# Half of the weight slabs cast straight from fp32 memory into the SBUF ring, with loads issued five slabs ahead

## The chip, the cores and the metric

The kernel runs on all 8 cores of one Trainium2 chip, one batch element on each core. The metric is the device time of the slowest core in microseconds (us), as the median of several executions. Most executions of one kernel agree within a fraction of a per cent. Some fall into a second, slower state, in which the cores of one die show a lower granted TensorE clock and the time is some per cent longer. A stage is read from the trace of one profiled execution, and where one core of it is named, from that core.

## The reference

The reference is one decoder layer on x of shape (8, 2048, 1024), with fp32 inputs and outputs. Each core gets one batch element, so 2048 rows of 1024.

```python
hcat = x @ w_in                                     # 7 groups of 512 columns
b_gate, c_gate, hc, q, k, v, g = split(hcat)
y_conv = b_gate * causal_short_conv(c_gate * hc, conv_w)
o      = chunkwise_retention(rotary(q), rotary(k) * 128**-0.5, v)   # 4 heads, 128 each
y_ret  = silu(g) * head_group_norm(o)
mix    = concat([y_conv, y_ret]) @ w_out            # 1024 x 1024
x      = layer_norm(alpha * x + mix)
ff     = square(relu(x @ w_ff1)) @ w_ff2            # 1024 x 4096, 4096 x 1024
ple    = sigmoid(x @ w_ple_gate) * (p @ w_ple_proj)
x      = layer_norm(alpha * x + ff + ple)
```

## The kernel before

The program has a conv stage, a retention stage of 18 steps, and then four tiles of 512 rows. A tile runs ff1 (8 weight slabs), gate (2 slabs), the output projection "mix" of the next tile (2 slabs of w_out) and ff2 (8 slabs). A slab is a [128, 8, 512] block of weights: 1 MiB in bf16, 2 MiB in fp32. TensorE works in bf16 and the weights arrive in fp32, so before any slab is loaded, the kernel casts it once from fp32 DRAM to bf16 DRAM scratch. Only DMAs that GpSimd issues (the software queue) cast here; SP issues plain loads (the hardware queue).

```python
casts = []                                   # 20 DRAM-to-DRAM casts, issued by GpSimd
for g in range(2): casts.append((s_wout[g], w_out[g], ("c_wout", g), ("s_wout", g)))
# ... [cut: the same for 8 of ff1, 2 of gate, 8 of ff2]
issue_casts(4)                               # and then one after each retention step

NR = 6                                       # six slabs in the ring
def load_slab(src, rsrc):                    # issued by SP, in order, at the point of use
    i = rcnt[0] % NR
    rcnt[0] += 1
    h.dma("sp", ring[i][:], src, ("ring", i), [rsrc], [("ring", i)])
    return ring[i], ("ring", i)

def mix_part(tt, bi, hf, slab, rs, bank):    # x @ w_out for 128 rows, half the columns
    b = tt * 4 + bi
    i = xcnt[0] % 4                          # four xin buffers of 256 KB
    xcnt[0] += 1
    cols = slice(hf * 512, (hf + 1) * 512)
    h.dma("sp", xin[i][:], x[b * 128:(b + 1) * 128, cols], ("xin", i), [], [("xin", i)])
    for kc in range(8):
        h.mm(ps[bank][:], ycat[:, kc, blk(b)], slab[:, kc, :], kc == 0, kc == 7, ...)
    h.stt(x1v(tt, bi)[:, cols], xin[i][:], ALPHA, ps[bank][:], ALU.mult, ALU.add, ...)

for tt in range(4):
    phase_ff1(tt)
    bg.flush()
    phase_gate(tt)
    if tt < 3:
        phase_mix(tt + 1)                    # two halves hf, four blocks bi each
        bg.add(gen_norm1(tt + 1))            # LayerNorm and transposes, spread over ff2
    phase_ff2(tt)                            # uses the same PSUM banks ps[bi] as phase_mix
    # ... [cut]
```

Tile 0's own mix runs inside the retention stage, in steps 8 to 11, with its own eight xin loads. An xin buffer is loaded again only when VectorE's `stt` of four blocks earlier has read it. And ff2 writes the PSUM banks that the last `stt` of the mix must first have read.

## Time and profile before

The median was 900.96 us when the prediction was made. The profile is of core 0, 896.4 us. In what follows, a stage is bounded by the starts of TensorE's weight loads, counted from the first: all 4,088 are in every trace, in the same order of work, so the same count is the same point of the program.

| | before |
|---|---|
| PE busy | 807.7 us, 90% |
| retention stage (all 18 steps, with the first five ff1 groups) | 200.8 us |
| rest of ff1 of tile 0 | 60.2 us |
| last mix half before ff2, tiles 0, 1, 2 | 9.7, 9.5, 9.6 us |
| from the last matmul's weight load to the end | 19.3 us |

The page's busy time of TensorE (busy us, share of the span, instructions), and its table of DMA queues (packets, MB, share of the time of the 16 DMA engines). q0 is the queue of GpSimd and q1 that of SP:

```profile
PE 807.7 (90%) x4088; PEld 376.8 (42%) x4088; DVE 443.7 (49%) x696; ACT 276.8 (31%) x500; POOL 126.1 (14%) x165
...
q1 hardware_dynamic: 17280, 96.68, 32.9%
q0 software_dynamic: 5136, 41.42, 30.8%
```

TensorE bounds the kernel and has about 89 us of idle time; DMA engines are busy 64% on average. What TensorE waited for (us in total, times, longest us), on core 0:

```profile
PE psT L198 <- DVE ob_94 L201: 24.8, 7, 18.8
PE ps L194 <- DMA wc_59<-wc: 18.3, 1, 18.3
PE ps L194 <- DMA ring_108<-s_ff: 9.6, 2, 7.4
...
PE ps L194 <- DMA ring_106<-s_ff: 2.5, 1, 2.5
PE ps L194 <- DMA ring_104<-s_ff: 2.4, 1, 2.4
```

The 18.3 us is the start, which the change does not touch. The others are the gaps that it can touch: 18.8 us is the prediction's gap A, 7.4 us its gap B, and the 2.2 us beside it (9.6 in two waits), 2.5 and 2.4 us its gaps C. The largest is VectorE's, which works in order and waits for an x load. The timeline shows it (start us, us, engine, line, operation, and in brackets the idle time before it and what ended that):

```profile
116.93 0.95 SPq L236 DMA_DIRECT2D xin_115<-x  x1
...
213.16 0.69 DVE L212 SCALAR_TENSOR_TENSOR xacc_118<-xin_115,ps 128x512 f32<-128x512 f32 x1 [20.71 <-DMA xin_115<-x]
...
215.90 0.58 PE L198 MATMUL psT<-ident,ob_94 128*128 128x128 bf16 x4 [18.75 <-DVE ob_94 L201]
```

A load of 256 KB took from 116.9 to 213 us. Last, three windows at the end of tile 0's gate and mix, core 0 (window, its length, busy us and instructions of PE, PEld, DVE, ACT and POOL, granted clock, share of the DMA engines, GB/s):

```profile
338.00:365.00 27.00, 27.00 (x127) 12.21 (x125) 10.49 (x16) 9.55 (x16) 0.00 (x0) 1.00 0.82 278
365.00:383.00 18.00, 18.00 (x86) 8.16 (x84) 10.97 (x16) 6.21 (x10) 0.00 (x0) 1.00 0.00 1
383.00:400.00 17.00, 14.53 (x68) 6.47 (x67) 8.49 (x15) 0.45 (x1) 0.13 (x1) 1.00 0.56 163
```

Just before the mix the DMA engines do nothing at all (share 0.00): SP stands in its in-order queue before the x loads of the mix and issues nothing behind them. This is the DMA view of 365 to 420 us (KB each, us from issue to landing):

```profile
xin_114<-x SPq DMA_DIRECT2D x1, 256.0 KB, 2.9
xin_115<-x SPq DMA_DIRECT2D x1, 256.0 KB, 4.1
xin_116<-x SPq DMA_DIRECT2D x1, 256.0 KB, 3.8
xin_117<-x SPq DMA_DIRECT2D x1, 256.0 KB, 5.0
```

### The profile page before, as it was taken

The page shows a single profiled execution, that of the slowest core. Times are in us where ns is not written, and L with a number is a line of the kernel's source. Part 1 is how long each engine was busy: PE and PEld are TensorE (multiplying, and loading weights), DVE is VectorE, ACT ScalarE, POOL GpSimd, SP SyncE. Part 2 cuts the span into 40 slices and gives each one's busy share as a digit, 9 for nine tenths or more (in the row PEclk, how much of TensorE's full clock was granted, in tenths as well). Part 3 has the DMA queues.
Part 4 walks back from the last instruction along what each step waited for, and adds up shares of the span by engine and source line. Part 5 has one row for each costly group of instructions (what it writes and reads, how often), then busy time and mean ns, then how long its engine had stood idle before and what let it go on. Part 6 is the DMA issues. An engine that isn't in the chain of part 4 may idle for free.

```text
span 896.4 us, 12614 instructions; the slowest of 8 cores (879.0 to 896.4 us)
## 1 busy us (share of the span) xinstructions
PE 807.7 (90%) x4088; PEld 376.8 (42%) x4088; DVE 443.7 (49%) x696; ACT 276.8 (31%) x500; POOL 126.1 (14%) x165
## 2 busy tenths in 40 slices
PE   1999999973988869989999999999998999999991
PEld 0444444431444324434444443444443444444440
DVE  4559545522765323553358453427655344844143
ACT  2222235541666513302224311214430222432011
POOL 3000045631345300000001000001100000100001
PEclk9999999995999979999999999999999999999996
DMA  8999999994866999058446419435805744643201
GB/s 133 216 170 140 109 201 113 124 112 81 141 118 95 142 220 337 29 173 297 141 150 205 164 28 325 165 141 176 276 18 145 306 154 145 213 169 137 95 24 70
DMA packets 22479, 138.90 MB, mean 155 GB/s; under 512 B 2960, under 2 KB 3088, under 8 KB 10384
## 3 DMA queue, kind: packets, MB, share of 16 engines
q1 hardware_dynamic: 17280, 96.68, 32.9%
q0 software_dynamic: 5136, 41.42, 30.8%
q8 instruction: 34, 0.56, 0.3%
q14 instruction: 29, 0.24, 0.1%
HBM read 162.73 MB, written 29.36 MB: 214 GB/s over the span
## 4 chain that ended last, share of the span: by engine, by line
PE 73%; DMA 8%; DVE 5%; issue 4%; ACT 3%; POOL 3%; another core or an unknown queue 2%; SPq 0%; DVEq 0%; ACTq 0%; POOLq 0%
PE ps L194 71%; DMA ring_108<-s_ff 3%; DMA xT_56<-xT 3%; ACT sqj L223 2%; PE psT L198 1%; POOL st_51 L201 1%; DVE xacc_119 L201 1%; DVE lnst L645 1%; DMA ring_106<-s_ff 1%; DMA ring_104<-s_ff 1%; DVE ra_80 L201 1%; ACT xacc_119 L223 1%; DVE ob_93 L201 0%; DVE ob_94 L201 0%
## 5 line engine op out<-in xcount | busy, mean ns | idle before, releaser
L201 POOL TENSOR_TENSOR lnst<-lnst,neghalf 128x1 f32<-128x1 f32 x32 | 17.8, 556 | 461.7 <-DVE lnst L205 461.7
L223 ACT ACTIVATE xacc_119<-xacc_119,lnst 128x1024 f32<-128x1024 f32 x16 | 19.8, 1236 | 99.2 <-DVE lnst L212 99.2
L201 DVE TENSOR_TENSOR hT<-ps,tR_129 128x512 bf16<-128x512 f32 x42 | 28.9, 688 | 36.2 <-ACT tR_129 L223 36.1
L194 PE MATMUL ps<-ring_104,hT 128*128 128x512 bf16 x192 | 43.1, 379 | 2.4 <-DMA ring_104<-s_ff 2.4
L194 PE MATMUL ps<-ycat,ring_108 128*128 128x512 bf16 x160 | 38.1, 400 | 7.4 <-DMA ring_108<-s_ff 7.4
L201 DVE TENSOR_TENSOR hT<-ps,tR_128 128x512 bf16<-128x512 f32 x43 | 29.6, 689 | 30.3 <-ACT tR_128 L223 30.2
L194 PE MATMUL ps<-ycat,ring_107 128*128 128x512 bf16 x192 | 44.1, 386 | 0.0
L223 ACT ACTIVATE tR_129<-ps 128x512 f32<-128x512 f32 x42 | 25.1, 597 | 61.0 <-PE ps L194 57.5
L194 PE MATMUL ps<-ring_105,hT 128*128 128x512 bf16 x192 | 43.2, 379 | 0.0
L201 DVE TENSOR_TENSOR hT<-ps,tR_127 128x512 bf16<-128x512 f32 x43 | 29.6, 689 | 27.1 <-ACT tR_127 L223 25.6
L194 PE MATMUL ps<-ycat,ring_106 128*128 128x512 bf16 x192 | 42.9, 379 | 0.0
L223 ACT ACTIVATE tR_127<-ps 128x512 f32<-128x512 f32 x43 | 25.7, 597 | 54.3 <-PE ps L194 49.7
L223 ACT ACTIVATE tR_128<-ps 128x512 f32<-128x512 f32 x43 | 25.7, 597 | 53.1 <-PE ps L194 49.6
L194 PE MATMUL ps<-ring_108,hT 128*128 128x512 bf16 x160 | 37.7, 392 | 2.2 <-DMA ring_108<-s_ff 2.2
L194 PE MATMUL ps<-ring_106,hT 128*128 128x512 bf16 x160 | 35.5, 379 | 2.5 <-DMA ring_106<-s_ff 2.5
L201 DVE TENSOR_TENSOR xacc_119<-ps,xacc_119 128x512 f32<-128x512 f32 x16 | 11.0, 690 | 51.6 <-PE ps L194 51.5
L194 PE MATMUL ps<-ring_109,hT 128*128 128x512 bf16 x160 | 36.2, 379 | 0.0
L194 PE MATMUL ps<-ring_107,hT 128*128 128x512 bf16 x160 | 35.7, 379 | 0.0
L194 PE MATMUL ps<-ycat,ring_109 128*128 128x512 bf16 x160 | 35.3, 379 | 0.1
L194 PE MATMUL ps<-ycat,ring_105 128*128 128x512 bf16 x160 | 35.4, 379 | 0.0
L194 PE MATMUL ps<-ycat,ring_104 128*128 128x512 bf16 x160 | 35.3, 379 | 0.0
L223 ACT ACTIVATE ycat<-psT 128x1024 bf16<-128x1024 bf16 x16 | 16.3, 1020 | 58.4 <-PE psT L198 58.4
(254 smaller groups left out, 1440.9 us busy)
## 6 DMA issues: line engine op xcount, KB each, us to landing
s_ff<-w_ff POOLq DMA_DIRECT2D x16, 1024.0 KB, 17.4
ring_106<-s_ff SPq DMA_DIRECT2D x11, 1024.0 KB, 7.8
ring_107<-s_ff SPq DMA_DIRECT2D x11, 1024.0 KB, 7.0
ring_104<-s_ff SPq DMA_DIRECT2D x11, 1024.0 KB, 6.0
ring_105<-s_ff SPq DMA_DIRECT2D x11, 1024.0 KB, 5.4
ring_108<-s_ff SPq DMA_DIRECT2D x10, 1024.0 KB, 6.8
ring_109<-s_ff SPq DMA_DIRECT2D x10, 1024.0 KB, 6.3
out<-xacc_118 POOLq DMA_DIRECT2D x8, 512.0 KB, 6.2
```

Source lines behind the costliest of these rows:

```text
L194: self.P.op("pe", lambda e: e.matmul(out, lhsT=lhsT, rhs=rhs, start=start, stop=stop, skip_group_check=skip), reads, writes)
L198: self.P.op("pe", lambda e: e.transpose(out=out, in_=in_, identity=ident), reads, writes)
L201: self.P.op(eng, lambda e: e.tensor_tensor(out=out, in0=in0, in1=in1, op=op), reads, writes)
L223: self.P.op("act", lambda e: e.activation(out=out, in_=in_, func=func, **kw), reads, writes)
L645: P.op("dve", lambda e, hf=hf: e.bn_stats(out=st6[:, hf * 6:(hf + 1) * 6], in_=buf[:, hf * 512:(hf + 1) * 512]), [rbuf], [rl])
```

## The change

The intent was to halve the DRAM-to-DRAM casts and to keep the ring full. Half of the slabs (even ones) are now cast from fp32 DRAM straight into the ring by GpSimd in every tile. In tile 0 all of them are. Slabs are issued five ahead of their use. The x loads leave `mix_part` and are issued a little earlier: the first four of a tile at its gate stage, each further one when its buffer is free.

```diff
-        casts = []
-        for g in range(2):
-            casts.append((s_wout[g], w_out[g], ("c_wout", g), ("s_wout", g)))
-        ... [cut: ff1, gate, ff2; 20 in all]
+        slab_list = [("wout", g, 0) for g in range(2)]
+        for tt in range(4):
+            slab_list += [("ff1", g, tt) for g in range(8)]
+            slab_list += [("gate", g, tt) for g in range(2)]
+            if tt < 3:
+                slab_list += [("wout", g, tt + 1) for g in range(2)]
+            slab_list += [("ff2", g, tt) for g in range(8)]
+        casts = [(n, g) for n, c in (("ff1", 8), ("gate", 2), ("wout", 2), ("ff2", 8))
+                 for g in range(1, c, 2)]                       # 10 in all
+        def prefetch(upto):
+            while slab_n["load"] < min(upto, len(slab_list)):
+                ...
+                if tt > 0 and g % 2 == 1:
+                    h.dma("sp", ring[i][:], wsrc[nm][1][g], ("ringh", i), [("s_" + nm, g)],
+                          [("ring", i)])
+                else:
+                    cast(ring[i][:], wsrc[nm][0][g], ("ring", i), ("ring", i))
+        def use_slab(nm, g, ahead=5):
+            ...
+            prefetch(k + 1 + ahead)
+            return ring[slab_buf[k]], ("ring", slab_buf[k])
@@ mix_part
-            h.dma("sp", xin[i][:], x[b * 128:(b + 1) * 128, cols], ("xin", i), [], [("xin", i)])
...
+            if xn["use"] % 8 <= 4 and xn["use"] % 8 > 0:
+                load_xin(1)
@@ retention loop
-                slabs0 = [load_slab(s_wout[g], ("s_wout", g)) for g in range(2)]
+                slabs0 = [use_slab("wout", g, 0) for g in range(2)]
+                load_xin(4)
-            issue_casts(1)
+            if t % 2 == 0:
+                issue_casts(1)
@@ phase_gate
-                slab, rs = load_slab(s_gate[hf], ("s_gate", hf))
+                slab, rs = use_slab("gate", hf)
+                if hf == 0:
+                    load_xin(4)
@@ phase_mix, phase_ff1, phase_ff2: load_slab(...) becomes use_slab(...) [cut]
```

More of the change, by code (lines that the diff above doesn't have):

```diff
@@ L429, in build_nc @@
               [("wc", 1)], ["wVf"])
-        casts = []
-        for g in range(2):
-            casts.append((s_wout[g], w_out[g], ("c_wout", g), ("s_wout", g)))
-        for g in range(8):
-            casts.append((s_ff1[g], w_ff1[g], ("c_ff1", g), ("s_ff1", g)))
-        for g in range(2):
-            casts.append((s_gate[g], w_gate[g], ("c_gate", g), ("s_gate", g)))
-        for g in range(8):
-            casts.append((s_ff2[g], w_ff2[g], ("c_ff2", g), ("s_ff2", g)))
+        wsrc = dict(wout=(w_out, s_wout), ff1=(w_ff1, s_ff1), gate=(w_gate, s_gate),
+                    ff2=(w_ff2, s_ff2))
+        slab_list = [("wout", g, 0) for g in range(2)]
[5 more added lines that the diff above has]
+            slab_list += [("ff2", g, tt) for g in range(8)]
+        slab_buf = [0, 1, 2, 3, 0, 1, 4, 5]
+        while len(slab_buf) < len(slab_list):
+            slab_buf.append(slab_buf[-6])
+        casts = [(n, g) for n, c in (("ff1", 8), ("gate", 2), ("wout", 2), ("ff2", 8))
+                 for g in range(1, c, 2)]
         def issue_casts(n):
@@ L443, in issue_casts @@
                 if casts:
-                    cast(*casts.pop(0))
+                    nm, g = casts.pop(0)
+                    cast(wsrc[nm][1][g], wsrc[nm][0][g], ("c_" + nm, g), ("s_" + nm, g))
+        slab_n = {"load": 0, "use": 0}
+        def prefetch(upto):
+            while slab_n["load"] < min(upto, len(slab_list)):
+                k = slab_n["load"]
+                slab_n["load"] += 1
+                nm, g, tt = slab_list[k]
+                i = slab_buf[k]
+                if tt > 0 and g % 2 == 1:
[4 more added lines that the diff above has]
+        def use_slab(nm, g, ahead=5):
+            k = slab_n["use"]
+            slab_n["use"] += 1
+            assert slab_list[k][:2] == (nm, g), (slab_list[k], nm, g)
+            prefetch(k + 1 + ahead)
+            return ring[slab_buf[k]], ("ring", slab_buf[k])
         h.cp("dve", ident[:], identf, ["cst"], ["ident"])
@@ L517, in build_nc @@
         bg.flush()
-        issue_casts(4)
+        prefetch(3)
+        issue_casts(3)
         rot = [0]
@@ L662, in gen_ln, with load_xin @@
             yield
-        xcnt = [0]
+        xorder = [(bi, hf) for bi in range(4) for hf in range(2)]
+        xorder += [(4 * tt + bi, hf) for tt in range(1, 4) for hf in range(2) for bi in range(4)]
+        xn = {"load": 0, "use": 0}
+        def load_xin(k):
+            for _ in range(k):
+                if xn["load"] == len(xorder):
+                    return
+                b, hf = xorder[xn["load"]]
+                i = xn["load"] % 4
+                xn["load"] += 1
+                h.dma("sp", xin[i][:], x[b * 128:(b + 1) * 128, hf * 512:(hf + 1) * 512],
+                      ("xin", i), [], [("xin", i)])
         def x1v(tt, bi):
@@ L673, in mix_part @@
             b = tt * 4 + bi
-            i = xcnt[0] % 4
-            xcnt[0] += 1
+            i = xn["use"] % 4
+            assert xorder[xn["use"]] == (b, hf) and xn["use"] < xn["load"]
+            xn["use"] += 1
             cols = slice(hf * 512, (hf + 1) * 512)
-            h.dma("sp", xin[i][:], x[b * 128:(b + 1) * 128, cols], ("xin", i), [], [("xin", i)])
             for kc in range(8):
@@ L694, in x1_transpose @@
             h.cp("act", ycat[:, :, blk(b)], psT[:], [RT], [("ycat", b)])
-        rcnt = [0]
-        def load_slab(src, rsrc):
-            i = rcnt[0] % NR
-            rcnt[0] += 1
-            h.dma("sp", ring[i][:], src, ("ring", i), [rsrc], [("ring", i)])
-            return ring[i], ("ring", i)
         ff1 = {"n": 0, "slab": None}
@@ L708, in ff1_group @@
             if fc % 4 == 0:
-                ff1["slab"] = load_slab(s_ff1[fc // 4], ("s_ff1", fc // 4))
+                ff1["slab"] = use_slab("ff1", fc // 4, 5 if tt or fc > 4 else 0)
             slab, rs = ff1["slab"]
@@ L774, in build_nc @@
                 bg.add(chains[bi])
-            issue_casts(1)
+            if t == 12:
+                prefetch(6)
+            if t == 16:
+                prefetch(8)
+            if t % 2 == 0:
+                issue_casts(1)
         issue_casts(len(casts))
@@ L820, in phase_mix @@
             for hf in range(2):
-                slab, rs = load_slab(s_wout[hf], ("s_wout", hf))
+                slab, rs = use_slab("wout", hf)
                 for bi in range(4):
@@ L846, in phase_ff2 @@
                 if tt == 3 and hf == 1:
-                    slabs = [load_slab(s_ff2[4 + g], ("s_ff2", 4 + g)) for g in range(4)]
+                    slabs = [use_slab("ff2", 4 + g) for g in range(4)]
                     for bi in range(4):
@@ L855, in phase_ff2 @@
                 for g in range(4):
-                    slab, rs = load_slab(s_ff2[hf * 4 + g], ("s_ff2", hf * 4 + g))
+                    slab, rs = use_slab("ff2", hf * 4 + g)
                     for bi in range(4):
```

## The prediction

> **What bounds it now.** TensorE: busy 90% of 896.4 us (page, part 1), 73% of the chain of waits. A middle tile (446 to 594 us, windows view) has PE busy 145.8 of 148 us, so only gaps can be won. PE's waits on core 0 that the change can touch:
>
> - A: 18.8 us at 197 us. A PE transpose waits for ob_94 because VectorE, in order, waits 20.7 us for xin_115. That 256 KB load was issued at 116.9 us and landed at 213, behind two ring loads on its queue, while software-queue casts kept the DMA share at 1.03 (118 to 193 us). In 110 to 215 us the software queue moved 21 KB a packet (9.67 MB, 455 packets), the hardware queue 3.4 KB. The Trainium skill (DMA: Bandwidth & Descriptors, "Queues, rings and completion order") says each DMA engine round-robins between queues at packet granularity; 96 us for xin_115 agrees.
> - B: 7.4 us at 314 us: the third ff1 slab, issued only at 298.3, landed 22.8 us later behind the backlog.
> - C: 2.5, 2.2 and 2.4 us, one at each ff2 start. The ff2 loads stand behind eight xin loads in SP's in-order queue and go out 8 us before need.
>
> After a gap matmuls run 0.43 us apart instead of 0.216 (timeline, about 12 after B). The skill (TensorE: Matmul & The Clock Gate, "Part 1: The HAM clock gate") describes this half clock when cold. I add 3 us for B and 3 for A and C. Sum: 18.8 + 7.4 + 7.1 + 6 = 39 us on core 0. The same sum puts nearly every core near 855 to 858.
>
> **What the change does.** Removes 10 of 20 DRAM-to-DRAM casts, 9 to 10 us of DMA each (the s_wout casts landed at 86.4 and 96.3 us). Turns 50 of 80 slab loads into fp32 casts on GpSimd's queue: about 6.3 us each (landings of xT_57 to wK, 52.2 to 77.3 us for four), against 3.2 for a bf16 slab (part 3: 32.9% of 896 us for 96.7 MB). Estimate: -95 + 155 = +60 us of DMA work, share 64% to about 74%. None should be critical: PE uses a slab in 6.9 us, five are ahead. Tightest is tile 0: 18 casts x 6.3 = 113 us, plus about 18 for pT, wproj, ln2, xin = 131 of 147 us. Moved: xin goes ahead of need and no longer before ring loads; the wout slabs leave SP's queue; slab waits now sit in GpSimd's in-order stream beside the LayerNorm powers.
>
> **On the critical path:** A, B and C go. I charge 3 us for new waits. Start (18.3 us before the first matmul), conv stage, retention steps (about 9.4 us each) and the 30 us LayerNorm tail stay.
>
> **Predicted: 863 us, 80% range 852 to 880.** Faster by over 2%: 0.90; within 2%: 0.08; slower: 0.02.
>
> **Right if:** no VectorE wait for xin near 193 us, no PE wait for ring tiles at ff1 and ff2 starts, PE busy 93 to 94%, software-queue share up and hardware-queue share down, cores' spans closer together. **Wrong if:** PE waits for ring tiles in tile 0 (casts slower than 6.9 us with both cores of a pair reading 2 MB a slab); PE transposes wait on LayerNorm chains delayed at GpSimd; xin still lands after step 8 because the remaining casts saturate the queue; or the granted clock falls as PE becomes denser.

## The result and the profile after

The changed kernel took 892.9 us in the median of 10 runs, against 899.37 us in 20 runs of the kernel before (three slow runs are in the first median, one in the second). The ratio of the fast runs is 0.9922, with a 95% interval of 0.9901 to 0.9943. Such a ratio is the mean time of one kernel's fast runs over that of the other's of the same rounds, so it is not quite the ratio of the medians quoted. The change is real and under 1%, and outside the predicted range of 852 to 880. The profiled execution's slowest core is core 4, 891.7 us.

The ledger by stages shows that the expected gains came, nearly all of them, and that they were given back mostly in one place.

```
stage (us)                          before, core 0   after, core 4   difference
retention (gap A in it)                     200.8           180.1        -20.7
rest of ff1 of tile 0 (gap B in it)          60.2            54.4         -5.8
last mix half before ff2, tile 0              9.7            11.9         +2.2
                          tile 1              9.5             6.9         -2.6
                          tile 2              9.6             6.9         -2.7
first half of ff2, tile 0                    27.5            47.9        +20.4
                   tile 1                    29.2            29.3         +0.1
                   tile 2                    27.5            29.6         +2.1
last matmul's weight load to the end         19.3            22.2         +2.9
all other stages                            503.1           502.5         -0.6
span                                        896.4           891.7         -4.7
```

"First half of ff2" here means a fixed count of 140 weight loads from the start of ff2; a wait before the first of them counts to the mix. The table pairs the slowest core of each run. The mean of all eight cores has the same pattern (retention -19.5, rest of ff1 -5.4, first half of ff2 of tile 0 +17.7 us), but its span fell only from 888.7 to 886.7 us: the cores came closer together, from 879.0 to 896.4 us before to 881.6 to 891.7 after, so of the slowest core's 4.7 us only 2.0 are a gain of the mean; the rest is the narrower spread. The gaps had not been of one size before (retention 195.5 us on core 2, 200.7 on core 0). The page's lines that answer to those of before:

```profile
PE 805.7 (90%) x4010; PEld 375.9 (42%) x4088; DVE 443.7 (50%) x696; ACT 276.9 (31%) x500; POOL 147.6 (17%) x205
...
q0 software_dynamic: 11856, 83.37, 56.2%
q1 hardware_dynamic: 10080, 44.25, 15.1%
```

PE's share did not rise. (78 matmul records are missing from this core's trace, the weight loads are all there.) The software queue went from 30.8% to 56.2% of the DMA engines' time. TensorE's waits on core 4:

```profile
PE ps L194 <- DMA wc_59<-wc: 18.8, 1, 18.8
PE ps L194 <- DVE xacc_119 L212: 17.6, 5, 4.6
PE psT L198 <- DVE ob_94 L201: 5.6, 6, 2.9
...
PE ps L194 <- DMA ring_106<-w_ff: 2.0, 1, 2.0
```

The wait for ob_94 fell from 24.8 to 5.6 us, and the waits for ring tiles from 14.5 to about 4. A new line stands in their place: 17.6 us for VectorE's line 212, the `stt` of the mix. All eight cores show it (13.7 to 18.1 us). The timeline of core 4 shows what that `stt` waited for:

```profile
373.48 0.69 DVE L212 SCALAR_TENSOR_TENSOR xacc_119<-xin_114,ps 128x512 f32<-128x512 f32 x1 [6.02 <-DMA xin_114<-x]
374.31 3.57 PE L194 MATMUL ps<-ring_106,hT 128*128 128x512 bf16 x8 [4.61 <-DVE xacc_119 L212]
...
396.44 0.69 DVE L212 SCALAR_TENSOR_TENSOR xacc_119<-xin_117,ps 128x512 f32<-128x512 f32 x1 [7.32 <-DMA xin_117<-x]
...
397.27 3.57 PE L194 MATMUL ps<-ring_106,hT 128*128 128x512 bf16 x8 [4.54 <-DVE xacc_119 L212]
```

Four times in a row the first matmuls of ff2 wait for a PSUM bank, the bank waits for the `stt`, and the `stt` waits for an x load. The four x loads land 7.2 to 8.1 us apart (373.3, 381.0, 388.2, 396.3 us). After each wait the eight matmuls take about 3.5 us, 0.43 us apart instead of 0.216, so they run at half clock. The landings set the pace all the same: the first and the fourth group start 22.96 us apart, and so do the landings of their loads. Of the 20.4 us lost in the first half of ff2, 17.8 lie between these two groups (22.96 us for 24 matmuls that need 5.2 at 0.216 us each); the rest, 2.6 us, is about what the half clock costs after the fourth wait, where 13 matmuls ran 0.43 us apart. *TensorE: Matmul & The Clock Gate*, "Part 1: The HAM clock gate" of the Trainium skill says that the array runs at half clock until it has been busy for a few microseconds. The trace agrees: after the fourth wait it took 5.5 us. The same windows as before, now of core 4:

```profile
338.00:365.00 27.00, 26.43 (x121) 12.04 (x124) 13.67 (x20) 6.40 (x10) 2.11 (x4) 1.00 1.00 179
365.00:383.00 18.00, 9.30 (x32) 3.44 (x32) 2.06 (x3) 0.00 (x0) 0.53 (x1) 0.69 0.99 177
383.00:400.00 17.00, 8.68 (x21) 2.66 (x20) 3.12 (x7) 0.00 (x0) 0.56 (x1) 0.70 0.73 127
```

The DMA engines, idle here before, are now full (0.99), and TensorE is half idle at a mean granted clock of 0.7 (the records alternate between 0.5 and 1.0). The DMA view of 338 to 400 us:

```profile
q0 software_dynamic: 1131, 8.21, 79.4%
q1 hardware_dynamic: 1074, 1.94, 12.6%
...
xin_114<-x SPq DMA_DIRECT2D x1, 256.0 KB, 14.7
xin_115<-x SPq DMA_DIRECT2D x1, 256.0 KB, 20.6
xin_116<-x SPq DMA_DIRECT2D x1, 256.0 KB, 26.1
xin_117<-x SPq DMA_DIRECT2D x1, 256.0 KB, 28.7
```

The packet counts of the two queues are almost equal, 1131 and 1074. Their bytes are not: 8.21 and 1.94 MB. The trace's DMA records of this window give the sizes. The software queue's data packets write 8,192 bytes and take 0.785 us of a DMA engine; those of x write 2,048 bytes and take 0.128 us. A 256 KB x load is 128 packets, 8 on each of 16 engines if they are spread evenly. If each waits for one software packet, the load takes 8 x (0.785 + 0.128) = 7.3 us, close to the spacing seen (7.7 us on average). The records show the alternation itself. From 343 to 392 us, while x packets always wait, 847 cast packets and 856 x packets were carried, and on each of the eight cores the two counts are within 7%. The records do not name the engine, but their times pair up: about 85% of the x packets end within 5 ns before a cast packet starts, beyond what coincidence gives.

### The profile page after: what moved, and what is told of

It is laid out like the page before. It is cut to its first block, busy times and chain, and to the rows that moved or that the text cites. A ratio compares the mean times of both kernels' runs of the same rounds, so it can differ in the third digit from the quotient of the medians.

```text
span 891.7 us, 12485 instructions; the slowest of 8 cores (881.6 to 891.7 us)
## 1 busy us (share of the span) xinstructions
PE 805.7 (90%) x4010; PEld 375.9 (42%) x4088; DVE 443.7 (50%) x696; ACT 276.9 (31%) x500; POOL 147.6 (17%) x205
## 3 DMA queue, kind: packets, MB, share of 16 engines
q0 software_dynamic: 11856, 83.37, 56.2%
## 4 chain that ended last, share of the span: by engine, by line
PE 65%; DMA 12%; DVE 7%; issue 6%; ACT 4%; POOL 4%; DVEq 0%; SPq 0%; ACTq 0%; POOLq 0%
PE ps L194 64%; DMA xin_117<-x 11%; DMA wc_59<-wc 2%; ACT sqj L223 2%; DVE lnst L673 2%; POOL st_51 L201 1%; DVE xacc_119 L201 1%; PE psT L198 1%; DVE xacc_118 L201 1%; ACT xacc_119 L223 1%; POOL lnst L201 1%; DVE ra_80 L201 1%; ACT xacc_118 L223 1%; DVE ob_93 L201 0%; POOL kr_83 L201 0%
## 5 line engine op out<-in xcount | busy, mean ns | idle before, releaser
L194 PE MATMUL ps<-ring_106,hT 128*128 128x512 bf16 x156 | 42.4, 429 | 17.2 <-DVE xacc_119 L212 17.0
L194 PE MATMUL ps<-ycat,ring_107 128*128 128x512 bf16 x188 | 43.4, 385 | 1.2 <-DMA ring_107<-w_ff 1.0
L194 PE MATMUL ps<-ycat,ring_106 128*128 128x512 bf16 x186 | 42.4, 379 | 2.3 <-DMA ring_106<-w_ff 2.0
L194 PE MATMUL ps<-ring_108,hT 128*128 128x512 bf16 x189 | 42.8, 379 | 0.8 <-DVE xacc_119 L212 0.7
L194 PE MATMUL ps<-ring_109,hT 128*128 128x512 bf16 x188 | 42.5, 379 | 0.2
L223 ACT ACTIVATE tR_129<-ps 128x512 f32<-128x512 f32 x42 | 25.1, 597 | 53.1 <-PE ps L194 49.7
L194 PE MATMUL ps<-ring_107,hT 128*128 128x512 bf16 x157 | 36.6, 387 | 0.2
L194 PE MATMUL ps<-ring_104,hT 128*128 128x512 bf16 x156 | 36.0, 379 | 0.5 <-DVE xacc_118 L212 0.3
L194 PE MATMUL ps<-ycat,ring_104 128*128 128x512 bf16 x156 | 36.0, 385 | 0.2
L194 PE MATMUL ps<-ring_105,hT 128*128 128x512 bf16 x157 | 35.7, 379 | 0.2
L194 PE MATMUL ps<-ycat,ring_108 128*128 128x512 bf16 x158 | 35.2, 379 | 0.1
L194 PE MATMUL ps<-ycat,ring_105 128*128 128x512 bf16 x157 | 35.2, 379 | 0.2
L194 PE MATMUL ps<-ycat,ring_109 128*128 128x512 bf16 x157 | 35.0, 379 | 0.2
L194 PEld LDWEIGHTS ps<-ring_106,hT 128*128 128x128 bf16 x160 | 16.6, 106 | 41.4 <-issue 26.6
```

The costliest lines, as they stand in the source:

```text
L194: self.P.op("pe", lambda e: e.matmul(out, lhsT=lhsT, rhs=rhs, start=start, stop=stop, skip_group_check=skip), reads, writes)
L223: self.P.op("act", lambda e: e.activation(out=out, in_=in_, func=func, **kw), reads, writes)
```

## The experiments

**Theory T.** In tile 0 the software queue is never empty, because all 18 slabs (and the first w_out slab of the mix) are fp32 casts of 2 MiB. The DMA engines alternate between the two queues packet by packet, so a small-packet x load is slowed by the size of the other queue's packets. Since the second four x loads of a mix are issued only when the first four have been read, 7 us before need, they land late, and ff2 waits.

**Rival R.** Tile 0 has more bytes to move than DMA time, and whichever load is last is late. Then moving the x loads would only move the wait to a slab.

**Rival O.** GpSimd's in-order stream or the order of issue is at fault.

Twelve kernels ran, in three groups of four, each group on one chip with its own runs of the kernel before (medians 894.78, 908.61 and 897.0 us). All gave the right result. Stage times are those of the slowest core of the profiled execution, if not said otherwise; "tile 0" is the time from the end of the retention stage to the start of ff1 of tile 1 (150.9 us before, 167.6 after).

### 1. x straight into the accumulator

```diff
+        def load_xacc(tt):
+            for bi in range(4):
+                b = tt * 4 + bi
+                h.dma("sp", x1v(tt, bi), x[b * 128:(b + 1) * 128, :], ("xal", tt % 2, bi), [],
+                      [x1r(tt, bi)])
... [cut: mix_acc replaces mix_part for tiles 1 to 3, x1v = ALPHA * x1v + ps, no xin buffer]
+        load_xacc(1)                      # tile 1: right after the retention stage
@@ phase_gate
-                if hf == 0:
-                    load_xin(4)
+                if hf == 0 and 0 < tt < 3:
+                    load_xacc(tt + 1)
```

> Same bytes and the same GpSimd casts as the changed kernel; only x for tiles 1 to 3 goes straight into the accumulator, 512 KB a block, a whole stage before it is needed, so no x load is issued inside the mix. Theory T (the lost 20 us are small x loads taking turns, packet for packet, with a GpSimd queue that is never empty in tile 0): the first half of ff2 of tile 0 falls from 47.9 us to 27.5 to 30, the second mix half before it from 11.9 to 7, no VectorE wait for xin there; time about 866 us, 860 to 872. Rival R (tile 0 has too little DMA time for its bytes, whichever load is last is late): PE waits for ring tiles in tile 0 instead, time above 882. GpSimd's last drain stays 7.32 us (89 DMAs issued by GpSimd).

Measured: 872.98 us, ratio 0.9769 (0.9737 to 0.9802), so the verdict by the 2% rule is "unclear". First half of ff2 of tile 0 27.7 us, mix half before it 6.9 us, and 27.7 us in the other two tiles as well. That is T's number at T's place. But the total missed T's range by 1 us. The rest of ff1 of tile 0 took 61.7 us instead of 54.4, through one wait of TensorE:

```profile
PE ps L194 <- DMA ring<-w_ff: 10.8, 1, 10.8
```

So R has a share: 2 MB of x, put beside six slab loads, made one slab late. Experiments 9 and 10 tell how much of that was placing.

### 2. Odd slabs of tile 0 from scratch

```diff
-                if tt > 0 and g % 2 == 1:
+                if g % 2 == 1 and (tt > 0 or nm != "wout"):
```

> Odd slabs come from bf16 scratch in tile 0 too (9 fewer fp32 casts there), the x loads stay as in the changed kernel. T and R both expect the stall of ff2 of tile 0 to go or shrink: software queue's share at 338 to 400 us from 0.79 to 0.5 or less, xin landing in under 15 us instead of 15 to 44; first half of ff2 of tile 0 28 to 35 us; time 866 to 876. If GpSimd's in-order waits or the order of issue were the cause, this would not help: above 885. Drain 54 ns + 81.7 ns x 80 DMAs = 6.6 us.

Measured: 869.75 us, ratio 0.9722 (0.9669 to 0.9776). The software queue's share at 338 to 400 us fell from 79.4% to 48.3%; the second four x loads took 4 to 12 us. First half of ff2 of tile 0 30.6 us, tile 0 142.2 us. With half as many casts most of the stall goes, which T and R both expect. (The edit also halves GpSimd's slab issues in tile 0, so it does not rule out O by itself; experiment 3 speaks to that.) In each of the three tiles about 3 us stay (30.6, 31.0, 30.6 where 27.7 is possible), by x loads that are still issued 7 us before need.

### 3. The same bytes in smaller packets

```diff
-                    cast(ring[i][:], wsrc[nm][0][g], ("ring", i), ("ring", i))
+                    cast(ring[i][:, 0:4, :], wsrc[nm][0][g, :, 0:4, :], ("ring", i), ("ring", i))
+                    cast(ring[i][:, 4:8, :], wsrc[nm][0][g, :, 4:8, :], ("ringB", i), ("ringB", i))
... [cut: matmuls on the second half of a slab wait for ringB]
```

> Each fp32 slab cast is issued as two DMAs of half the columns: same bytes, software packets of 4 KB written instead of 8 KB. T (turn taking): a turn falls from 0.785 + 0.128 us to about 0.4 + 0.13, an xin load from 7.4 to about 4.3 us, so the ff2 stall of tile 0 falls from 20 us to 5 to 10. R (bytes): stall unchanged within 3 us. The 50 more GpSimd DMAs lengthen the last drain to 54 + 81.7 x 139 = 11.4 us. Time: T 880 to 887, R 893 to 898.

Measured: 879.28 us, ratio 0.9844 (0.9806 to 0.9881), just under T's range. The DMA view of 338 to 400 us on core 3:

```profile
q0 software_dynamic: 2656, 9.68, 94.2%
q1 hardware_dynamic: 838, 1.52, 9.0%
...
xin<-x SPq DMA_DIRECT2D x4, 256.0 KB, 12.8
```

The software queue is busier than in the changed kernel (94.2%) and moves more bytes, so by R nothing should improve. Its packets now take 0.394 us, and the four x loads land 3.5 to 4.7 us apart (366.9, 371.6, 375.1, 379.4). T's estimate was 4.3. First half of ff2 of tile 0 fell from 47.9 to 35.0 us, a stall of 7.5 us instead of 20.4. This is the run that shows turn taking by packets, rather than bytes, as the cause of the stall. From 362 to 378 us, with x waiting, 516 cast packets and 505 of x were carried; from 346 to 360 us, with no x waiting, 580 and 1. It also has twice as many slab issues by GpSimd, and the stall shrank, which speaks against GpSimd's stream (rival O). What is true of O is that the x loads are issued late, which T contains. The drain did not come out as expected: 9.61 us, not 11.4 (see below).

### 4. All slabs from scratch, in the new order

```diff
-                 for g in range(1, c, 2)]
+                 for g in range(c)]
-                if tt > 0 and g % 2 == 1:
+                if nm != "wout" or tt > 0:
-        prefetch(3)
-        issue_casts(3)
+        issue_casts(4)
+        prefetch(3)
-            if t % 2 == 0:
-                issue_casts(1)
+            issue_casts(1)
```

> The changed kernel's order, prefetch and xin loads, but all slabs after the first two from bf16 scratch, so all 20 DRAM-to-DRAM casts. Tile 0 then has almost no software-queue work: xin lands in 3 to 7 us, first half of ff2 of tile 0 27.5 to 29, later ff2 starts without a DMA wait. The DRAM-to-DRAM casts (32 KB packets, 4.5 us each) fill the retention stage again: if they are what delayed xin there, the stage takes 190 to 201 us as before; if the order of SP's queue was, 180 to 183. Drain 4.2 us (51 DMAs). Time 865 to 880.

Measured: 884.06 us, ratio 0.9895 (0.986 to 0.993), slower than expected. Tile 0 is the shortest of all (137.9 us; first half of ff2 27.7 us, x loads landing in 2.7 to 6.3 us). The gaps C are gone (6.9 us in all three tiles) though every slab comes from scratch, so C was a matter of order and not of the source. (The first two w_out slabs are still casts.) The retention stage took 207.8 us, 7 us longer than even the kernel before: its first x load was issued at 107 us and landed at 198.

### 5. Twenty casts in the changed kernel

```diff
-                 for g in range(1, c, 2)]
+                 for g in range(c)]            # the ten more results are never read
-        issue_casts(3)
+        issue_casts(4)
-            if t % 2 == 0:
-                issue_casts(1)
+            issue_casts(1)
```

> The changed kernel with all 20 DRAM-to-DRAM casts, one a retention step, the 10 extra results never read; slab loads, order and x loads stay. If it is halving the casts that removed the 18.8 us stall of the retention stage: x for the first mix lands late again, stage 195 to 210 us instead of 180, and the total 15 to 30 us above the changed kernel. If it is the order of SP's queue (x ahead of the slab loads): stage 180 to 184, total within 5 us but for the drain (54 ns + 81.7 ns x 99 DMAs = 8.14 us, 0.8 longer).

Measured: 970.18 us, ratio 1.0704 (1.0639 to 1.0769). The retention stage took 233.4 us. The direction is the expected one; the size was underestimated. The first four x loads were issued at 106.5 to 108.6 us, as in the changed kernel, and landed at 144.9, 176.5, 206.1 and 235.5 us: 30 us apart, for as long as the casts lasted. In the changed kernel the first two landed at 144.0 and 174.2 and the next two together at 192, when the casts had run dry. They were needed at 191, 192, 206 and 207 us. A DRAM-to-DRAM cast has packets of 32,768 bytes that take 4.5 us; eight turns in 30 us are 3.7 us each, less than one such packet: here the turns are not one for one. From 176.5 to 206 us one x load's 128 packets passed beside 96 cast packets, and over the last three of these loads about a quarter of the x packets followed another x packet at once. So halving the casts is what removed gap A, and it did so by little: the same turn taking ended just in time. The retention stage is not all of the loss: the rest of ff1 of tile 0 took 77.5 us (54.4 in the changed kernel), with two waits of 17.0 and 8.5 us for fp32 slabs.

### 6. Both repairs together

The edits of 1 and 2.

> The two repairs together: x of tiles 1 to 3 straight into the accumulator, and odd slabs of tile 0 from scratch. The first lost 7.3 us in ff1 of tile 0 by a wait for one slab (10.8 us), the second 3 us in each of three ff2 stages by late x loads. Theory T: both go; retention stage 180 us, ff1 of tile 0 50 to 52, every first half of ff2 27.5 to 28, no PE wait for a ring tile over 2 us; drain 6.59 us; time 859 to 864. Rival R (what is saved in one place comes back in another, since the bytes are short of time): time stays at 868 or more.

Measured: 890.1 us, ratio 0.9812 (0.9732 to 0.9892), "unclear", on a chip where the kernel before took 908.61. In the profiled execution cores 6 and 7 had a clock of 0.95 and spans of 887 to 889 us, the other six 871.6 to 873.4 us. The second run counted as fast has the same on cores 4 and 5, so this ratio is not of undisturbed runs. On core 4 every first half of ff2 was 27.7 us, as expected, but the rest of ff1 of tile 0 took 64.2 us. The expectation failed there, for a reason in my edit:

```profile
PE ps L194 <- DMA ring<-s_ff: 9.3, 1, 9.3
```

The x loads of tile 1 were put into SP's in-order queue ahead of the odd slabs of tile 0, which now also go through SP. It is defect C again, made by hand. Experiments 9 to 11 mend it.

### 7. The kernel before with x straight into the accumulator

The first edit of experiment 1, on the kernel before.

> The kernel before with one change: x of tiles 1 to 3 straight into the accumulator; all slabs from scratch and loaded at the same points of SP's stream. If the gaps C came from slab loads standing behind x loads in SP's queue: the three ff2 starts (9.7, 9.5, 9.6 us) fall to 6.9 and the first halves of ff2 stay at 27.5, so about 8 to 10 us less than the kernel before; the stall of 18.8 us in the retention stage and the wait of 7.4 us in ff1 of tile 0 stay within 5 us. Time 884 to 890 where the kernel before has 895. Drain 4.06 us.

Measured: 918.03 us, ratio 1.0041 (0.9964 to 1.0119). Two of the four runs were slow; the fast ones took 909.96 and 910.38 us. The three mix halves before ff2 fell to 6.9 us as expected, and the first halves of ff2 were 27.7. The rest of ff1 of tile 0 grew to 79.4 us (core 0) by a wait of 28.4 us for a ring tile, for the reason found in 6. The expected total failed for it.

### 8. Stores on SP

Experiment 6 with the output stores issued by SP.

```diff
-            h.dma("pool", out[b * 128:(b + 1) * 128, :], x1v(tt, bi), ("outq", bi),
+            h.dma("sp", out[b * 128:(b + 1) * 128, :], x1v(tt, bi), ("outq", bi),
```

> As acc_half, with the 16 output stores issued by SP instead of GpSimd: 64 GpSimd DMAs instead of 80. If the last drain of GpSimd costs 54 ns + 81.7 ns for each DMA that GpSimd issued: 5.28 us instead of 6.59, and the time 1 to 2 us below acc_half; 858 to 863. If stores on SP's in-order queue hold up slab loads, PE waits for ring tiles at the starts of tiles and the time is above acc_half.

Measured: 880.45 us, ratio 0.9636 (0.9561 to 0.971), where two of four runs were at 873 us and two, slow, at 887. The rest of ff1 of tile 0 is as bad as in 6 (65.1 us). The drain was 5.28 us as expected, and the stage from the last matmul to the end 19.7 us against 22.5 in experiment 6. Of those 2.8 us the drain explains 1.3. The other 1.5 lie before it: the last store was issued 0.6 us earlier and the drain began 14.2 us after the last matmul's weight load instead of 15.7.

### 9. Experiment 1 with x of tile 1 issued later

```diff
-        load_xacc(1)                      # after the retention stage
@@ ff1_group
+            if ff1["n"] == 16:
+                load_xacc(1)
```

> As x_in_acc (slab sources of the changed kernel, x of tiles 1 to 3 into the accumulator), but x of tile 1 is issued halfway through ff1 of tile 0 instead of right after the retention stage, where it took turns with six slab loads and cost 7.3 us. Theory T: ff1 of tile 0 back to 51 to 55 us, mix and ff2 of tile 0 stay at 6.9 and 27.7, so the 25 us come back with the changed kernel's own bytes: slowest core 863 to 867. Rival R (18 fp32 slabs are too many bytes for tile 0): PE waits for ring tiles later in tile 0 instead, the sum of tile 0's stages stays above 148 us (it was 142 at best, 168 in the changed kernel).

Measured: ratio 0.9707 (0.9637 to 0.9776). Three of its five runs fell in the slow state, so the median of 914.29 us says nothing; the fast ones were 867.23 and 869.04 us. Slowest core 867.5 us, half a microsecond over the range. Tile 0 took 146.1 us, below R's 148 and 21.5 us less than in the changed kernel, with the same slab sources and the same bytes. Rest of ff1 57.9 us (expected 51 to 55), through a wait of 6.7 us for one fp32 slab. So of the 29.7 us by which the changed kernel's tile 0 exceeds that of experiment 4 (167.6 against 137.9), the x loads account for 21.5, and 8.2 remain with 18 fp32 slabs in that tile (slowest cores; by the mean of eight cores 20.4 of 27.0, and 6.6 remain).

### 10. Experiment 6 with x of tile 1 issued later

The edits of 1, 2 and 9.

> acc_half with the same delay of x of tile 1. acc_half lost 13 us in ff1 of tile 0 (64.2 instead of 51) because x went ahead of the odd slabs in SP's queue. Now ff1 of tile 0 50 to 52, all else as in acc_half: slowest core 859 to 862 in an undisturbed run.

Measured: 864.72 us, ratio 0.9669 (0.9623 to 0.9716). Slowest core 864.7 us, 3 us above the range: on core 0 the rest of ff1 of tile 0 took 54.7 us with a wait of 3.4 us for an fp32 slab, on core 1 49.9 us, with a span of 858.0.

### 11. The best version: the same with stores on SP

The edits of 1, 2, 8 and 9.

> As acc_half_late with the output stores on SP: last drain 5.28 us instead of 6.59, and the stage from the last matmul to the end 19.7 us as it was in acc_half_spout against 22.5 in acc_half; slowest core 856 to 860. If stores on SP hold up slab loads, a stage of a later tile grows.

Measured: 861.75 us, ratio 0.9633 (0.9564 to 0.9702), so it beats both kernels. Slowest core 859.5 us, drain 5.29 us, end stage 19.7 us. Its page:

```profile
PE 799.7 (93%) x4088; PEld 374.7 (44%) x4088; DVE 443.5 (52%) x696; ACT 276.8 (32%) x500; POOL 133.9 (16%) x180
...
q0 software_dynamic: 8256, 65.54, 47.7%
q1 hardware_dynamic: 11952, 62.07, 20.8%
```

This is the profile that the prediction had described for the change (863 us, PE 93 to 94%). The change alone does not reach it.

### 12. Experiment 7 with x issued behind the slab loads

```diff
-        load_xacc(1)                      # after the retention stage
-                if hf == 0 and 0 < tt < 3:
+                if hf == 0 and tt < 3:
                     load_xacc(tt + 1)
```

> The kernel before with x of tiles 1 to 3 into the accumulator, but issued at the gate stage, behind the ff1 slab loads (before_acc put it ahead of them and lost 15 to 19 us in ff1 of tile 0). ff2 starts 6.9 us instead of 9.5 to 9.7, first halves of ff2 27.5 to 27.7; retention stage and ff1 of tile 0 as in the kernel before (196 to 201 and 57 to 60). 8 to 10 us less than the kernel before.

Measured: 889.72 us, ratio 0.9928 (0.9874 to 0.9982), about 7 us less than the kernel before, by the medians, where 8 to 10 were expected. Mix halves before ff2 6.9 us, first halves of ff2 27.7 us, retention stage 199.3 us; rest of ff1 of tile 0 62.6 us, a little above the 57 to 60 expected. This confirms C by itself.

### GpSimd's last drain

The end stage grew by 2.9 us. The trace has one record there that changed much: GpSimd's last DRAIN, which all engines wait for (prof does not list it; it is read from the instruction records). In all 14 kernels it begins after the last store has landed and the span ends 0.23 us after it. In the changed kernel it is 3.27 us longer and begins 0.39 us sooner, which is the 2.9 us. It is the same on all cores of a kernel.

```
DMAs issued by GpSimd   drain, us   kernel
 49                       4.057     before, experiments 7 and 12
 51                       4.221     experiment 4
 64                       5.282     experiment 8 (5.287 in experiment 11)
 80                       6.589     experiments 2, 6 and 10
 89                       7.324     after, experiments 1 and 9
 99                       8.141     experiment 5
139                       9.611     experiment 3 (half-size casts)
```

The first six rows follow 54 ns + 81.7 ns x DMAs within 5 ns. The law was fitted to the first and the fifth and then stated before the others ran. The seventh does not follow it (11.4 was expected); whether smaller DMAs cost less or a limit is reached was not tested.

## Why the prediction was wrong

- **Gap A (18.8 us), right.** The retention stage fell by 20.7 us. The prediction listed "xin still lands after step 8 because the remaining casts saturate the queue" as a risk; the last of the four landed at 192.2 us and was needed at 207, and experiment 5 shows the risk come true at 20 casts.
- **Gap B (7.4 us and 3 for the clock), partly.** The stage fell by 5.8 us. Fresh short waits for fp32 slabs (2.0, 1.0 and 0.9 us on core 4) took some of it back.
- **Gaps C, right in tiles 1 and 2, wrong in tile 0.** The mix halves fell to 6.9 us in tiles 1 and 2 and rose to 11.9 in tile 0. That C was the order in SP's queue is shown by experiments 4 and 12.
- **The step that failed** is, in the prediction's words, "None should be critical: PE uses a slab in 6.9 us, five are ahead", with "I charge 3 us for new waits". Measured, the new waits cost 20.4 us in the first half of ff2 of tile 0 and 4.7 us in the mix before it (11.9 where 7.2 was implied by the removal of 2.5), and 2.1 us in tile 2. The slabs themselves were nearly in time, as predicted. What was late were the x loads, which had only been entered as DMA time in a sum ("about 18 for pT, wproj, ln2, xin"). "xin goes ahead of need" held only for the first four of a tile: the second four are issued one mix half before their use, and in tile 0 they stood behind the first four, of which the last landed at 366.6 us. In the kernel before they landed in 3 to 5 us, with the DMA engines idle just before and no packet of the software queue beside them; the change filled that time with 8 KB packets, and each of eight x packets on every engine waits for one, 7.7 us a load. The prediction had named the mechanism for gap A (packet turns, 96 us for one x load) and did not apply it to the stage that the change was about to saturate. Experiments 1 and 9 (x loads taken out of the mix) and 2 (fewer casts) remove the stall or most of it; 3 (smaller packets, same bytes) shrinks it to 7.5 us, within the 5 to 10 that this gives.
- **"Tile 0: 131 of 147 us"** was an average with too little margin, and its terms were too small. It left out the mix's w_out slabs (one cast, one plain load), and in the changed kernel the casts of 338 to 398 us landed 7.4 us apart, not 6.3, with the x packets between theirs. With x out of the way, 18 fp32 slabs still cost tile 0 up to 8.2 us (experiment 9 against experiment 4), of which 6.7 us are one wait for a slab.
- **Its other tests.** No VectorE wait for x is left near 193 us, the queues' shares moved as said, and the cores' spans came closer together. PE stayed at 90% where 93 to 94 were expected.
- **A term that was missing:** the end stage, which the prediction let stay, grew by 2.9 us, and GpSimd's drain by 3.27 us, with 40 more DMAs issued by GpSimd.
- **"Wrong if PE transposes wait on LayerNorm chains delayed at GpSimd":** that wait appears (2.0 us for x1b_53 on core 4), but experiments 1 and 9, with all of GpSimd's slab issues in place, have no such wait among their largest and 27.7 us in each ff2 half. So it came from the late `stt`, not from GpSimd.
- **The granted clock** did not fall as a state: 0.972 to 0.979 on the profiled cores against 0.97 to 0.98 before.

The sum is then: 39 us of gains expected on core 0 (before the 3 us charged for new waits), and 20.4 (ff2 of tile 0) + 4.7 (the mix before it) + 4.6 (gap B, 10.4 expected and 5.8 found) + 2.9 (the end) + 2.1 (tile 2) = 34.7 us not gained or given back. That leaves 4.3 us; the profiled pair shows 4.7.

## What to carry to other kernels

Before filling idle DMA time, look up which small, late-issued loads lived from that idle time: work out their landing from the number of packets per DMA engine times the other queue's packet time, and not from bytes. (That gave 4.3 and 7.3 us where 4.2 and 7.7 were measured; beside the 32 KB packets it gives 37 us, an estimate from 8 x (4.5 + 0.128), where 30 were measured.) Give every load on the path the same lead as the bulk loads, by giving it a destination that is free early (here the accumulator itself) and a place in its queue behind what is needed first. Placing matters as much as lead: the same x loads, issued half a stage too early, put waits of 9 to 11 us into ff1 of tile 0 in experiments 1, 6 and 8, and made that stage 19 us longer in experiment 7.

## What the Trainium skill lacked or had wrong

- *DMA: Bandwidth & Descriptors*, "Queues, rings and completion order" says that a DMA engine round-robins between queues at packet granularity. The runs agree (847 and 856 packets of the two queues from 343 to 392 us in the changed kernel). It does not say what follows for a small load beside a large one: a 256 KB load of 2,048-byte packets took 7.7 us a piece beside 8,192-byte cast packets, 4.2 us beside 4,096-byte ones and 30 us beside the 32,768-byte packets of DRAM-to-DRAM casts, where the turns were not one for one (128 to 96).
- The same page, "SWDGE vs HWDGE vs iDMA", gives a packet as "≤4096 B preferably". The records of casts in these traces, which took turns one for one with those of x, write 8,192 bytes (0.785 us) into SBUF; those into DRAM write 32,768 bytes (4.5 us).
- The same page has no figure for a DMA that casts: 1 MiB of bf16 from 2 MiB of fp32 landed every 6.3 us in the start-up queue (four of them in 25.1 us), and a DRAM-to-DRAM cast of the same size about every 10 us (86.5, 96.3, 106.9, 116.8).
- No page that I looked up has the cost of GpSimd's drain at the end of a program: 54 ns + 81.7 ns for each DMA that GpSimd issued, for 49 to 99 DMAs; 9.61 us at 139 half-size ones does not fit.
